# Chunk sums and outputs of an S5 scan: which operand is stationary

## The chip, the cores and the metric

The kernel runs on one core of a Trainium2 chip. The metric is device time in microseconds, from one launch to its end; a kernel's time is the median of several runs.

## The reference

A trunk of two layers works on 256 tokens of width 2048. Each layer normalises the stream, projects it, and feeds four branches: an S5 state-space layer (A), a gated DeltaNet (B), grid attention (C) and cross-attention into 256 memory tokens (M). Each branch is gated, projected back and merged; one output projection and a residual add end the layer.

The S5 branch has 48 groups of 16 channels, each with 64 complex states, and runs over the tokens forwards and backwards:

```
bu = einsum("blgp,gnp->blgn", u, bb)            # complex: bb_re, bb_im
s  = associative_scan(s_t = lam * s_(t-1) + bu_t, reverse=reverse)
y  = einsum("blgn,gpn->blgp", s_re, c_re) - einsum("blgn,gpn->blgp", s_im, c_im)
...
y = y_forward + y_backward + d * u
y = gelu(y);  y = y * sigmoid(y @ w_glu + b_glu)
```

## The kernel before

**The stream of large matmuls.** Most of the time goes to weight matrices that come from memory in chunks of 128 x 1024 (512 KB). Each chunk is split into a high and a low part, the high part by ScalarE (`hiN`, `hiT`) and the low part by VectorE (`loN`, `loT`), and TensorE multiplies three combinations of high and low parts into an accumulator (`acc`). Units of kind N have 512 moving columns and units of kind T have 256. The splits are issued two chunks ahead (`AHEAD = 2`), and a list (`ORDER`) fixes the sequence of the units in each layer.

**The order around it.** All engines get their instructions in an order worked out when the program is built. Small pieces of work are generators ("fibers"). After every few large matmuls, `tick` (line 530) lets those fibers go on whose data are ready by a model clock; `_time` (line 393) is the price list of that clock. On the chip each engine then works its own list in order and waits on semaphores.

**S5 in chunks.** The 256 tokens are cut into 32 chunks of 8. A group's 16 channels and 8 tokens make 128 rows, so that `ut` holds for each of 48 groups a 128 x 32 tile (rows by chunks). Twelve blocks have four groups each. The fiber `s5_fiber` (line 1458) goes through these steps in each layer:

1. `chunk_sums` (line 1473): for each block, the contribution of every chunk to the states: 128 rows of `ut` against a 128 x 256 matrix `W` for each group (64 states, two directions, real and imaginary parts), loaded from `Bd`. The result is copied into `Sx`, the states.
2. A recurrence over the 32 chunks on VectorE.
3. `outputs` (line 1524): for each block and group, three 128 x 128 matrices: `ct[0]` and `ct[1]` (loaded from `Cd`) meet the states `sy`, and `w0` (loaded from `Wd`) meets `ut`; the sum is copied to `yo`.
4. `yo` goes through memory into another layout, then GELU, and the units of the GLU, whose operand is called `sy` too.

Before the change the chunks are the stationary operand, 32 columns wide, and four groups share the array in four column tiles (`tile_position=(0, 32 * g)`), each writing 32 partitions of a PSUM bank; the matrices stream as the moving operand, 256 columns in the chunk sums and 128 in the outputs. So chunks come out on partitions. ScalarE copies the bank to a scratch tile, TensorE transposes it (`T`, line 662; two transposes for a block of chunk sums, one for a block of outputs), and ScalarE copies the transposed bank to `Sx` or `yo`.

In the profile all instructions bear line 379, where a helper records them, so they are told apart by their tiles. Both matmuls with `ut` appear as `bank<-scr,s5u`, those of the outputs with the states as `bank<-scr,scr`, transposes as `bank<-consts,...`. The DeltaNet's and S5's preparation use `bank<-scr,scr` and `bank<-scr,UA` too.

Of the kernel before, what the change touches and what calls it, by code (L numbers as in the profile page):

```python
# [11 lines left out]
AF = mybir.ActivationFunctionType  # L12
# [404 lines left out]
class Builder:  # L417
# [1040 lines left out]
    def s5_fiber(self, l):  # L1458
        nc = self.nc
        V, S, PE = self.V, self.S, self.PE  # L1460
        aux = 1 - l % 2
        yield from self.wait(("u", l))
        yield from self.wait(("pM", l))
        yield from self.wait(("C", l))
        yield from self.wait(("prep", l))
        Sx = self.slot(f"act{aux}0", "s5s", [128, 2, G_SSM, 33])
        ut = self.slot(f"act{aux}2", "s5u", [128, G_SSM, 32])
        for j in range(8):
            nc.sync.dma_start(out=ut[16 * j:16 * j + 16], in_=self.Ud[:, j, :].rearrange("(g i) c -> i g c", i=16))
        V.memset(Sx[:, :, :, 0:1], 0.0)  # L1470
        yield 7

        def chunk_sums(blocks):

            for b in blocks:
                gs = slice(4 * b, 4 * b + 4)
                W = yield from self.take(self.scr, 2)
                for hf in range(2):
                    nc.sync.dma_start(out=W[hf], in_=self.Bd[b][:, hf])
                yield 4  # L1480
                bank = yield from self.get(self.banks)
                for g in range(4):
                    PE.matmul(bank[32 * g:32 * g + 32, 0:256], ut[:, 4 * b + g, :], W[g // 2][:, (g % 2) * 256:(g % 2 + 1) * 256],
                              start=True, stop=True, tile_position=(0, 32 * g))
                self.scr.put(W[1])
                e = W[0]
                yield 1
                S.activation(out=e[:, 0:256], in_=bank[:, 0:256], func=AF.Copy)
                self.banks.put(bank)
                yield max(0, self.LAG + 1)  # L1490
                bank = yield from self.get(self.banks)
                for i in range(2):
                    self.T(bank[:, 128 * i:128 * i + 128], e[:, 128 * i:128 * i + 128])
                self.scr.put(e)
                yield 1
                src = bank[:, 0:256].rearrange("p (r g c) -> p r g c", r=2, c=32)
                S.activation(out=Sx[0:64, :, gs, 1:33], in_=src[0:64], func=AF.Copy)
                S.activation(out=Sx[64:128, :, gs, 32:0:-1], in_=src[64:128], func=AF.Copy)
                self.banks.put(bank)
                self.done(("sums", l))  # L1500

        self.expect(("sums", l), 12)
        for i in range(3):
            self.spawn(chunk_sums(range(i, 12, 3)))
        yield from self.wait(("sums", l))

        t = yield from self.get(self.scr)
        v = [t[:, 96 * i:96 * i + 96].rearrange("p (r g) -> p r g", r=2) for i in range(2)]
        tt = lambda o, a, b, op: V.tensor_tensor(out=o, in0=a, in1=b, op=op)
        lre, lim = self.lam8[:, 0:1, :].to_broadcast([128, 2, G_SSM]), self.lam8[:, 1:3, :]  # L1510
        for c in range(31):
            s0, s1 = Sx[:, :, :, c], Sx[:, :, :, c + 1]
            tt(v[0], s0, lre, ALU.mult)
            tt(v[1], s0[:, ::-1], lim, ALU.mult)
            tt(s1, s1, v[0], ALU.add)
            tt(s1, s1, v[1], ALU.add)
            yield 0
        self.scr.put(t)
        self.mark(("states", l))

        yo = self.slot(f"act{aux}3", "s5o", [128, G_SSM, 32])
        self.expect(("yo", l), 12)

        def outputs(blocks):
            for b in blocks:
                gs = slice(4 * b, 4 * b + 4)
                *ct, w0, w1 = yield from self.take(self.scr, 4)
                nc.sync.dma_start(out=w0, in_=self.Wd[:, 0, gs, :].rearrange("p g c -> p (g c)"))
                nc.sync.dma_start(out=w1, in_=self.Wd[:, 1, gs, :].rearrange("p g c -> p (g c)"))
                for i in range(2):  # L1530
                    nc.sync.dma_start(out=ct[i], in_=self.Cd[b][:, i])
                yield 6
                V.tensor_tensor(out=w0, in0=w0, in1=w1, op=ALU.add)
                sy = w1[:, 0:256].rearrange("p (r g c) -> p r g c", r=2, g=4)
                S.activation(out=sy[0:64], in_=Sx[0:64, :, gs, 0:32], func=AF.Copy)
                S.activation(out=sy[64:128], in_=Sx[64:128, :, gs, 31::-1], func=AF.Copy)
                yield self.LAG
                bank = yield from self.get(self.banks)
                for i in range(3):
                    for g in range(4):  # L1540
                        a = sy[:, i, g] if i < 2 else ut[:, 4 * b + g]
                        m = (ct[0], ct[1], w0)[i][:, g * 128:(g + 1) * 128]
                        PE.matmul(bank[32 * g:32 * g + 32, 0:128], a, m, start=i == 0, stop=i == 2, tile_position=(0, 32 * g))
                self.scr.put(*ct, w0)
                yield 0
                y1 = w1[:, 256:384]
                S.activation(out=y1, in_=bank[:, 0:128], func=AF.Copy)
                self.banks.put(bank)
                yield self.LAG
                bank = yield from self.get(self.banks)  # L1550
                self.T(bank[:, 0:128], y1)
                self.scr.put(w1)
                yield 1
                S.activation(out=yo[:, gs], in_=bank[:, 0:128].rearrange("p (g c) -> p g c", c=32), func=AF.Copy)
                self.banks.put(bank)
                self.done(("yo", l))

        self.spawn(outputs(range(0, 12, 2)))
        yield 6
        self.spawn(outputs(range(1, 12, 2)))  # L1560
        yield from self.wait(("yo", l))
        yield 1
        for j in range(8):
            nc.sync.dma_start(out=self.Yd[:, j, :].rearrange("(g o) c -> o g c", o=16), in_=yo[16 * j:16 * j + 16])
        yield 4

        Y = self.slot(f"act{aux}2", "s5y", [128, 6, 256])
        sy = self.slot(f"act{aux}0", "sy", [128, 6, 2, 256], F32R)
        nc.sync.dma_start(out=Y, in_=self.Yd.rearrange("(m p) j c -> p m (j c)", p=128))
        V.tensor_scalar(out=self.hbg, in0=self.sm(l, "b_glu"), scalar1=0.5, scalar2=None, op0=ALU.mult)  # L1570
        yield 8
        def gelu(m):
            s = yield from self.get(self.scr)
            y = Y[:, m:m + 2, :].rearrange("p m c -> p (m c)")
            S.activation(out=s, in_=y, func=AF.Square)
            yield 3
            V.tensor_scalar(out=s, in0=s, scalar1=0.044715, scalar2=1.0, op0=ALU.mult, op1=ALU.add)
            tt(s, s, y, ALU.mult)
            yield 3
            S.activation(out=s, in_=s, func=AF.Tanh, scale=math.sqrt(2.0 / math.pi))  # L1580
            yield 1
            V.scalar_tensor_tensor(out=y, in0=s, scalar=1.0, in1=y, op0=ALU.add, op1=ALU.mult)
            self.scr.put(s)
            yield 2
            S.activation(out=sy[:, m:m + 2, 0, :], in_=Y[:, m:m + 2, :], func=AF.Copy, scale=0.5)
            yield 5
            V.scalar_tensor_tensor(out=sy[:, m:m + 2, 1, :], in0=Y[:, m:m + 2, :], scalar=0.5,
                                   in1=sy[:, m:m + 2, 0, :].bitcast(F32), op0=ALU.mult, op1=ALU.subtract)
            self.done(("gelu", l))

        self.expect(("gelu", l), 3)
        for m in range(0, 6, 2):
            self.spawn(gelu(m))
        yield from self.wait(("gelu", l))
        self.sY = Y
        self.acts[("sy", l)] = [sy[:, 0:4], sy[:, 4:6]]
        self.expect(("A", l), 3)
        self.mark(("sy", l, 0))
        self.mark(("sy", l, 1))
        if l + 1 < DEPTH:  # L1600
            yield from self.wait(("B", l))
            self.spawn(self.s5_prep(l + 1), self.PREP_RANK[1])
# [276 lines left out]
```

## Time and profile before

| | us |
|---|---|
| median of 3 runs | 2280.83 (2280.21 to 2281.92) |
| the profiled run, its own time | 2280.38 |
| span of the profiled run, first to last instruction | 2278.6 |
| TensorE busy | 2228.1 |
| VectorE busy | 1700.7 |
| ScalarE busy | 1242.9 |
| mean granted clock of TensorE | 0.995 |

The busy time of an engine is the union of its instructions' times. Matmuls overlap their neighbours: the record of one begins before the one ahead of it has ended, so what a matmul costs is read from the distance between starts. PE is TensorE's matmul, PEld its weight load, DVE VectorE, ACT ScalarE.

### The profile page before, as it was taken

Reading aid. Unit: us, or ns where it says so; the run is one execution under the profiler, and the core shown is the slowest. Engines: PE = TensorE matmul, PEld = TensorE weight load, DVE = VectorE, ACT = ScalarE, POOL = GpSimd, SP = SyncE. Lnnn points to the kernel's source line nnn. Section 1 sums busy time; section 2 is a strip of 40 time slices with the busy share of each in tenths; the row PEclk is TensorE's granted clock in tenths of the full one; section 3 lists DMA queues with packets and bytes.
Section 4 is the critical chain, followed back from the end, with each engine's and each line's share of the span. In section 5 each row is a group of like instructions: output and inputs, shape, how many; then the busy total and the mean of one; then the engine's idle time right before and its main releaser. Section 6 shows DMA issues by size and latency. Waiting matters only on the chain.

```text
span 2278.6 us, 39516 instructions
## 1 busy us (share of the span) xinstructions
PE 2228.1 (98%) x14684; PEld 1930.3 (85%) x14684; DVE 1700.7 (75%) x2824; ACT 1242.9 (55%) x2176; POOL 89.8 (4%) x153
## 2 busy tenths in 40 slices
PE   6999999999999999999999999999999999999997
PEld 6988988988988888798789988898888887989886
DVE  6898887867859955889788858788646995566664
ACT  7645566465464454655665555666446445455443
POOL 0000000001000000000000000100000000000000
PEclk9999999999999999999999999999999999999999
DMA  6776678655775597778776786545478557877774
GB/s 247 250 246 214 229 247 280 203 189 190 183 264 197 185 322 259 252 230 293 266 228 206 244 288 210 191 169 205 166 196 279 199 197 277 263 253 258 231 245 139
DMA packets 245135, 523.42 MB, mean 230 GB/s; under 512 B 59320, under 2 KB 111032, under 8 KB 244304
## 3 DMA queue, kind: packets, MB, share of 16 engines
q1 hardware_dynamic: 218400, 471.41, 62.6%
q10 hardware_dynamic: 21952, 36.80, 4.5%
q0 software_dynamic: 4592, 12.69, 1.7%
q8 instruction: 117, 1.92, 0.3%
q14 instruction: 74, 0.61, 0.1%
HBM read 468.21 MB, written 65.18 MB: 234 GB/s over the span
## 4 chain that ended last, share of the span: by engine, by line
PE 89%; DVE 4%; DMA 2%; ACT 2%; issue 1%; SPq 0%; POOL 0%; ACTq 0%; POOLq 0%; DVEq 0%
PE acc L379 80%; PE bank L379 10%; DVE loT L379 2%; DVE hT L379 1%; DVE scr L379 1%; DMA Cd<-scr 1%; SPq L379 0%; DMA s5y<-Yd 0%; DVE dnx L379 0%; DMA xm<-x 0%; ACT hiT L379 0%; ACT scr L379 0%; DMA scr<-oTC 0%; DMA rawT<-wpack 0%; DMA Bd<-scr 0%
## 5 line engine op out<-in xcount | busy, mean ns | idle before, releaser
L379 ACT ACTIVATE hiN<-rawN 128x1024 fp32r<-128x1024 f32 x480 | 508.3, 1060 | 508.8 <-PE acc L379 431.5
L379 DVE TENSOR_TENSOR loN<-rawN,hiN 128x1024 fp32r<-128x1024 f32 x480 | 584.0, 1220 | 267.5 <-ACT hiN L379 266.1
L379 PE MATMUL acc<-hiN,xT 128*128 128x512 f32 x2432 | 619.3, 394 | 1.7 <-DVE hT L379 1.7
L379 PEld LDWEIGHTS acc<-hiN,xT 128*128 128x128 f32 x2432 | 449.6, 188 | 96.8 <-issue 5.9
L379 PE MATMUL acc<-xT,hiT 128*128 128x256 f32 x3392 | 444.8, 281 | 9.7 <-ACT gt L379 3.8
L379 PEld LDWEIGHTS acc<-xT,hiT 128*128 128x128 f32 x3392 | 413.3, 189 | 21.3 <-issue 11.3
L379 DVE TENSOR_TENSOR loT<-rawT,hiT 128x1024 fp32r<-128x1024 f32 x240 | 288.5, 1207 | 156.0 <-ACT hiT L379 151.4
L379 ACT ACTIVATE hiT<-rawT 128x1024 fp32r<-128x1024 f32 x240 | 250.3, 1048 | 182.6 <-PE acc L379 131.1
L379 PE MATMUL acc<-loN,xT 128*128 128x512 f32 x1216 | 337.1, 393 | 0.0
L379 PEld LDWEIGHTS acc<-loN,xT 128*128 128x128 f32 x1216 | 225.0, 188 | 46.3 <-issue 1.2
L379 PE MATMUL acc<-xT,loT 128*128 128x256 f32 x1696 | 239.6, 281 | 0.0
L379 PEld LDWEIGHTS acc<-xT,loT 128*128 128x128 f32 x1696 | 215.1, 190 | 2.6 <-issue 2.5
L379 ACT ACTIVATE scr<-bank 128x128 f32<-128x128 f32 (+6 forms) x324 | 105.7, 333 | 146.1 <-PE bank L379 122.6
L379 PE MATMUL acc<-hiN,y 128*128 128x512 f32 x640 | 161.5, 393 | 0.8 <-DVE scr L379 0.8
L379 PEld LDWEIGHTS acc<-hiN,y 128*128 128x128 f32 x640 | 118.5, 188 | 27.0 <-ACT hiN L379 1.8
L379 PE MATMUL acc<-hiN,mT 128*128 128x512 f32 x512 | 129.7, 393 | 1.3 <-ACT hiN L379 1.3
L379 DVE TENSOR_TENSOR dnx<-dnx 32x30 f32<-32x30 f32 (+9 forms) x360 | 114.6, 318 | 10.0
L379 PEld LDWEIGHTS acc<-hiN,mT 128*128 128x128 f32 x512 | 94.9, 188 | 21.5 <-ACT hiN L379 1.8
L379 PE MATMUL acc<-loN,y 128*128 128x512 f32 x320 | 88.7, 393 | 0.0
L379 DVE TENSOR_TENSOR scr<-scr,scr 128x512 f32<-128x512 f32 (+4 forms) x132 | 77.4, 590 | 2.4
L379 DVE SCALAR_TENSOR_TENSOR hT<-acc,small,hT 128x254 f32<-128x254 f32 (+1 forms) x144 | 69.1, 480 | 3.8
L379 PE MATMUL acc<-loN,mT 128*128 128x512 f32 x256 | 70.5, 393 | 1.3 <-DVE loN L379 1.3
(187 smaller groups left out, 2155.3 us busy)
## 6 DMA issues: line engine op xcount, KB each, us to landing
rawN<-wpack SPq DMA_DIRECT2D x480, 512.0 KB, 3.9
rawT<-wpack SPq DMA_DIRECT2D x234, 512.0 KB, 4.2
Bd<-scr ACTq DMA_DIRECT2D x48, 256.0 KB, 4.4
Cd<-scr SPq DMA_DIRECT2D x48, 256.0 KB, 4.7
Wd<-Kd SPq DMA_DIRECT2D x32, 384.0 KB, 6.1
scr<-Bd SPq DMA_DIRECT2D x48, 256.0 KB, 5.7
scr<-Wd SPq DMA_DIRECT2D x48, 256.0 KB, 5.1
scr<-Cd SPq DMA_DIRECT2D x48, 256.0 KB, 5.6
```

The costliest lines, as they stand in the source:

```text
L379: o = f(*args, **kw)
```

## The change

In both steps the operands change places. The matrices become the stationary operand, 128 columns wide on the full array, and the 32 chunks of a group the moving operand. The chunk sums take eight matmuls for a block instead of four, the outputs twelve as before; each writes 32 columns of a bank over all 128 partitions. The result then has the layout of `Sx` and `yo`: the copy to scratch, the transposes and the second bank go, and scratch tiles are given back right after the matmuls. The copies into `Sx` and `yo`, the loads and everything else stay.

```diff
                 bank = yield from self.get(self.banks)
                 for g in range(4):
-                    PE.matmul(bank[32 * g:32 * g + 32, 0:256], ut[:, 4 * b + g, :], W[g // 2][:, (g % 2) * 256:(g % 2 + 1) * 256],
-                              start=True, stop=True, tile_position=(0, 32 * g))
-                self.scr.put(W[1])
-                e = W[0]
-                yield 1
-                S.activation(out=e[:, 0:256], in_=bank[:, 0:256], func=AF.Copy)
-                self.banks.put(bank)
-                yield max(0, self.LAG + 1)
-                bank = yield from self.get(self.banks)
-                for i in range(2):
-                    self.T(bank[:, 128 * i:128 * i + 128], e[:, 128 * i:128 * i + 128])
-                self.scr.put(e)
+                    for i in range(2):
+                        PE.matmul(bank[:, (4 * i + g) * 32:(4 * i + g + 1) * 32],
+                                  W[g // 2][:, (g % 2) * 256 + 128 * i:(g % 2) * 256 + 128 * i + 128], ut[:, 4 * b + g, :],
+                                  start=True, stop=True)
+                self.scr.put(*W)
                 yield 1
...
                 bank = yield from self.get(self.banks)
-                for i in range(3):
-                    for g in range(4):
+                for g in range(4):
+                    for i in range(3):
                         a = sy[:, i, g] if i < 2 else ut[:, 4 * b + g]
                         m = (ct[0], ct[1], w0)[i][:, g * 128:(g + 1) * 128]
-                        PE.matmul(bank[32 * g:32 * g + 32, 0:128], a, m, start=i == 0, stop=i == 2, tile_position=(0, 32 * g))
-                self.scr.put(*ct, w0)
-                yield 0
-                y1 = w1[:, 256:384]
-                S.activation(out=y1, in_=bank[:, 0:128], func=AF.Copy)
-                self.banks.put(bank)
-                yield self.LAG
-                bank = yield from self.get(self.banks)
-                self.T(bank[:, 0:128], y1)
-                self.scr.put(w1)
+                        PE.matmul(bank[:, 32 * g:32 * g + 32], m, a, start=i == 0, stop=i == 2)
+                self.scr.put(*ct, w0, w1)
                 yield 1
```

## Rows read from the trace of the kernel before

**Rows 1.** The page's busy table: busy us, share of the span, instructions.

```profile
PE 2228.1 (98%) x14684; PEld 1930.3 (85%) x14684; DVE 1700.7 (75%) x2824; ACT 1242.9 (55%) x2176; POOL 89.8 (4%) x153
```

**Rows 2.** The chain that ended last, shares of the span by engine.

```profile
PE 89%; DVE 4%; DMA 2%; ACT 2%; issue 1%; SPq 0%; POOL 0%; ACTq 0%; POOLq 0%; DVEq 0%
```

**Rows 3.** Busy by stretch, clock, DMA: chunk sums, four S5 stretches' sum, 622 us.

```profile
632.00:676.00 44.00, 44.00 (x418) 37.13 (x417) 19.93 (x37) 31.66 (x82) 3.02 (x3) 1.00 0.80 272
...
sum 255.00, PE 252.26 PEld 215.13 DVE 136.88 ACT 153.94 POOL 6.43; mean PE 63.06 PEld 53.78 DVE 34.22 ACT 38.49 POOL 1.61
...
622.00:632.00 10.00, 7.43 (x124) 6.83 (x125) 7.84 (x14) 6.64 (x17) 0.00 (x0) 0.66 0.88 315
```

**Rows 4.** Waits of TensorE: us in total, times, longest us.

```profile
PE bank L379 <- ACT scr L379: 3.3, 3, 2.4
```

**Rows 5.** Timeline of TensorE at a block of chunk sums: start us, us.

```profile
1736.94 1.07 PE L379 MATMUL acc<-xT,loT 128*128 128x256 f32 x8
1737.85 0.38 PE L379 MATMUL bank<-consts,scr 128*128 128x128 f32 x2
...
1739.95 0.40 PE L379 MATMUL acc<-xT,loT 128*128 128x256 f32 x2
1740.28 0.64 PE L379 MATMUL bank<-scr,s5u 128*32 128x256 f32 x8
1740.85 0.96 PE L379 MATMUL acc<-xT,loT 128*128 128x256 f32 x6
1741.64 0.38 PE L379 MATMUL bank<-consts,scr 128*128 128x128 f32 x2
```

**Rows 6.** Timeline of TensorE at a block of outputs.

```profile
825.78 1.30 PE L379 MATMUL acc<-hiN,y 128*128 128x512 f32 x5
826.91 0.39 PE L379 MATMUL acc<-loN,y 128*128 128x512 f32 x1
827.23 0.64 PE L379 MATMUL bank<-scr,scr 128*32 128x128 f32 x16
827.69 0.40 PE L379 MATMUL bank<-scr,s5u 128*32 128x128 f32 x8
828.02 0.96 PE L379 MATMUL acc<-loN,y 128*128 128x512 f32 x3
828.82 0.27 PE L379 MATMUL bank<-consts,scr 128*128 128x128 f32 x1
```

**Rows 7.** Timeline of TensorE where only large matmuls run.

```profile
700.24 1.98 PE L379 MATMUL acc<-hiN,xT 128*128 128x512 f32 x8
702.05 1.07 PE L379 MATMUL acc<-loN,xT 128*128 128x512 f32 x4
```

**Rows 8.** Groups by form, matmuls: busy us, mean ns of one, idle before.

```profile
L379 PE MATMUL bank<-scr,UA 128*128 128x128 f32 x192 | 24.5, 276 | 0.0
L379 PE MATMUL bank<-hT 128*128 128x512 f32 x48 | 22.6, 592 | 0.0
...
L379 PE MATMUL bank<-scr,s5u 128*32 128x256 f32 x192 | 15.7, 390 | 1.9 <-DMA scr<-Bd 1.9
```

**Rows 9.** Groups by form, weight loads.

```profile
L379 PEld LDWEIGHTS bank<-consts,scr 128*128 128x128 f32 x388 | 46.8, 140 | 13.5 <-issue 2.8 <-ACT scr L379 2.3 <-DVE scr L379 1.0
...
L379 PEld LDWEIGHTS bank<-scr,UA 128*128 128x128 f32 x192 | 23.7, 191 | 1.4 <-ACT scr L379 0.2 <-issue 0.2
...
L379 PEld LDWEIGHTS bank<-scr,s5u 128*32 128x32 f32 x384 | 9.8, 109 | 5.7 <-DMA scr<-Bd 2.5 <-issue 1.2
```

**Rows 10.** Timeline of TensorE, sixteen float32 passes on the full array.

```profile
641.98 1.95 PE L379 MATMUL bank<-scr,UA 128*128 128x128 f32 x16
```

**Rows 11.** Timeline of TensorE, the first large matmuls after a wait (in brackets).

```profile
919.40 2.09 PE L379 MATMUL acc<-hiN,y 128*128 128x512 f32 x8 [0.82 <-DVE scr L379]
```

**Rows 12.** The GLU's operand, layer 0: ns min/median/max, first and last start.

```profile
L379 PE MATMUL acc<-sy,hiT x72: 276/276/386, 949.5 to 962.5; 128*128 128x256 f32 x72
...
L379 DVE SCALAR_TENSOR_TENSOR sy<-s5y,sy x3: 683/684/686, 928.8 to 940.2; 128x512 fp32r<-128x512 f32 x3
```

## The prediction

> **What bounds the kernel now.** I read the page's busy table first. TensorE is the engine to look at: busy 2228 of 2278.6 us [rows 1]. A busy share can hide a waiting engine, so the next view is the chain that ended last: 89% of it is TensorE [rows 2]. Then the four stretches in which the change lives (chunk sums and outputs, each in two layers). Over their 255.0 us TensorE is busy 252.3 us, ScalarE, which loses work in this change, 153.9 us [rows 3]: there are 2.7 us, no more, in which added TensorE work could disappear. The list of waits agrees: of TensorE's waits the one that the removed steps could have caused, on a scratch tile that ScalarE writes, is 3.3 us in the whole run, 2.4 us of it in one piece [rows 4]. So the question is only how much TensorE time a block of four groups takes before and after. Time that TensorE gains or loses here goes to the end of the kernel nearly one for one.
>
> **What a block costs now.** The reader should not add up durations, because these overlap; the cost of a small group is what it adds to the stream of large matmuls around it. In the chunk sums [rows 5]: from 1739.95 to 1741.64 are 1.69 us, which hold 2 + 6 large matmuls and one group of chunk sums (eight records). The eight large matmuls from 1736.94 to 1737.85 without a group take 0.91 us. The group costs 1.69 - 0.91 = 0.78 us. The eight records last 0.64 us together and one lasts 0.39 us [rows 5, 8], so they start within 0.25 us, and more than half of the price is getting into and out of the four column tiles. The two transposes last 0.38 us together and one lasts 0.27 us [rows 5, 6], so one comes 0.11 us behind the other; two cost 0.22 us. In the outputs [rows 6]: from 825.78 to 828.82 are 3.04 us with 5 + 1 + 3 large matmuls and one group (16 + 8 records). Large matmuls with 512 columns step at (702.05 - 700.24) / 8 = 0.226 us [rows 7], nine of them 2.04 us; the group costs 1.00 us, its one transpose 0.11 us. Together a block costs 0.78 + 0.22 + 1.00 + 0.11 = 2.11 us, and the 24 blocks (12 in each layer) 50.6 us. All of that goes.
>
> **What a block costs after.** Chunk sums: 4 groups x 2 halves = 8 matmuls with a 128-column stationary operand and 32 moving columns. Outputs: 4 x 3 = 12 of them. One float32 matmul is two records of weight load and stream: 2 layers x 12 blocks x 4 = 96 matmuls of the chunk sums stand as 192 records [rows 8]. So there are 16 + 24 = 40 passes a block, 960 in all. No row shows a pass with 128 stationary and 32 moving columns, and its price decides everything.
> From below, its stream: a float32 record of 512 columns takes 592 ns, one of 128 columns 276 ns [rows 8], which is 0.82 ns a column and 26 ns for 32 columns. Before it stands its weight load. Loads of 128 columns take 191 ns and loads of 32 columns 109 ns [rows 9]: 0.85 ns a column, so 128 columns occupy the load path for some 109 ns, the rest being latency. That a load really costs this when no stream covers it is seen after a wait: eight large matmuls last 2.09 us there and 1.98 us elsewhere [rows 11, 7], 0.11 us more. From above: the nearest row has the same stationary operand and four times the moving columns, 16 passes in 1.95 us, so one every (1.95 - 0.276) / 15 = 0.112 us [rows 10]; a pass with fewer columns can't be slower, unless load and stream stop overlapping. I take 0.112 us: at 128 columns load (0.109) and stream (0.105) are equally long, and shortening the stream leaves the load. 40 x 0.112 = 4.48 us a block, 107 us for all.
> The Trainium skill, "TensorEngine Tiling (Array Packing)", section Instruction Overhead, speaks the other way: a matmul has about 60 cycles of overhead, so that one with few columns costs what 60 columns cost. At 2.4 GHz that is an estimate of 25 ns a pass, by which the time would come out near 2253 us; it does not count the weight load, and no row here shows a pass so short with 128 stationary columns. The same page, section Performance Considerations, advises for at most 32 columns to make the narrow side stationary and to tile the columns, which is what the change undoes; the two prices here, 2.11 and 4.48 us a block, are on its side.
>
> **The rest of the change.** ScalarE loses two copies a block (a 128x256 and a 128x128 one); it has room in all four stretches, so this is worth nothing but the wait above, at most 3.3 - 2.4 = 0.9 us [rows 3, 4]; I take 0.5 us. The loads of the next block are issued when scratch tiles come back, and these come back earlier, since no copy and transpose hold one; nothing is added to SP's queue. A copy out of PSUM now waits for the longer group, and behind it on ScalarE stand the splits of the weights, on which TensorE waits in turn; they are issued two chunks ahead, and one chunk lasts 12 x 0.226 = 2.7 us of TensorE, so a delay of some 1 us a group is covered. Without that cover it would be up to 1 us for each of 48 groups. The next thing that could be late is the GLU, which waits for the outputs: its operand is ready at 940.2 + 0.7 us and its first matmul starts at 949.5 us [rows 12], and the work between is TensorE's own, so a longer TensorE stage moves both. The plan by which the program orders its instructions prices a new matmul at 0.08 us (line 393), so a block at 0.64 + 0.96 us instead of 0.67 + 0.83 us; the order should change little, and I allow 10 us to either side for it.
>
> **Sum.** The profiled run took 2280.38 us, 1.8 us more than its span, and the median is 0.45 us above it. 2280.4 - 50.6 + 107.1 - 0.5 = 2336.4 us, so 2336 us, slower by 2.4%. With passes at 0.109 us it is 2334 us.
>
> **Rivals.**
> Short streams win, faster than before: if a load were taken ahead while earlier passes run, so that loads no longer follow each other one at a time, a pass would cost its stream, 26 ns. Then 960 x 0.026 = 25 us replace 50.6 us: 2254 us. It decides below 2.11 / 40 = 53 ns a pass. For it: a load is seen to run beside a stream, since both fill the 0.112 us of a pass [rows 10]. Against it: the 0.11 us after a wait [rows 11], and that a load grows with its columns [rows 9]. Chance 0.03. The skill's rule on overhead, above, ends in the same place.
> Loads as short as those of the transposes: these take 140 ns, not 191 [rows 9], so 51 ns less, 58 ns a pass. 960 x 0.058 = 55.7 us: 2285 us, about the bound of what can be told. Against it: the transposes are another kind of matmul, the plain ones all show about 190 ns. Chance 0.05.
> Load and stream one after the other, 109 + 26 = 135 ns: 129.6 us, 2359 us. Against it: at 128 columns they overlap, or the 16 passes would take twice as long [rows 10]. Chance 0.05.
> The clock falls: TensorE's granted clock was at 0.66 in the ten microseconds from 622 us [rows 3], after waits, that is 6.8 us at 1.2 instead of 2.4 GHz and 3.4 us lost. Passes that stream for 26 of 112 ns leave the array idle for most of some 2 us at a time. One such spell for every two blocks of outputs would cost 12 x 3.4 = 41 us: 2377 us. Against it: between the groups stand full matmuls, and the clock read 1.00 all through the chunk sums of layer 0 [rows 3]. Chance 0.03.
> That it does nothing would need idle TensorE time to take it in, and there are 2.7 us [rows 3].
>
> **How the numbers follow.** The forecast has a chance of 0.84, with a range of its own from 2324 to 2350 us (0.109 to 0.115 us a pass and 10 us for the order). The faster rival is 0.03, and a shift of the order on top of the cheap loads adds 0.01 to faster and 0.02 to same; a difference under 0.2%, 4.6 us, cannot be told. Slower holds the rest, 0.94. The range goes from 2322 us to 2359 us, up to the serial case, and leaves out the two short-pass cases, the clock and a tail of the forecast, together some 0.17.
>
> **What the profile after would show.** Rows of TensorE with 128 stationary and 32 moving columns, 384 with the chunk operand and 384 with the states, stepping at 0.11 us; 16 of them 1.8 us, 24 of them 2.7 us. The rows with 32 stationary columns and 256 moving ones gone, transposes of scratch tiles down from 388 to 316. The stretches of chunk sums longer by about 0.8 us a block and those of outputs by 1.6 us, TensorE's waits no longer than now, the granted clock at 1.00 in them. A step of 0.03 or 0.06 us between these passes, a low clock in the stretches, or new waits for the weight splits would make the prediction wrong.

## The result and the profile after

The changed kernel takes 2332.66 us, the median of 4 runs (2331.24 to 2335.05), beside 2280.52 us for the kernel before (4 runs): a ratio of 1.0234, interval 1.0222 to 1.0247, so 52.1 us or 2.3% slower. The run that was profiled took 2331.24 us, its span is 2329.5 us and the mean granted clock 0.995.

The page of the changed kernel, first the busy table (busy us, share of the span, instructions), then the shares of the chain that ended last, answers to [rows 1, 2]:

```profile
PE 2283.4 (98%) x14804; PEld 2010.9 (86%) x14804; DVE 1699.9 (73%) x2824; ACT 1232.6 (53%) x2128; POOL 88.3 (4%) x153
...
PE 91%; DVE 4%; DMA 2%; ACT 2%; issue 1%; SPq 0%; ACTq 0%; POOL 0%; POOLq 0%; DVEq 0%
```

TensorE is busy 55.3 us longer than before and the span is 50.9 us longer. ScalarE lost 10.3 us of work, and the end moved the other way. The groups by form (busy us, mean ns of one, idle before) show the passes that have come in [rows 8, 9]:

```profile
L379 PE MATMUL bank<-s5u,scr 128*128 128x32 f32 x576 | 82.2, 273 | 0.6 <-DMA scr<-Bd 0.6
L379 PE MATMUL bank<-scr,scr 128*128 128x32 f32 x384 | 56.8, 271 | 0.0
L379 PE MATMUL bank<-consts,scr 128*128 128x128 f32 x316 | 49.2, 274 | 0.9 <-DVE scr L379 0.7 <-DVE memT L379 0.2
L379 PEld LDWEIGHTS bank<-s5u,scr 128*128 128x128 f32 x576 | 73.9, 192 | 0.9 <-DMA scr<-Bd 0.7
```

576 + 384 = 960 passes, and 72 transposes fewer (388 to 316). The mean of one, 273 ns, is no price: 960 of them would be 261 us. The price is in the starts. The timeline of TensorE at one block of chunk sums, and at one of outputs (start us, us, instruction, count), answers to [rows 5, 6]:

```profile
662.41 0.39 PE L379 MATMUL acc<-xT,loT 128*128 128x256 f32 x2
662.64 1.87 PE L379 MATMUL bank<-s5u,scr 128*128 128x32 f32 x16
664.34 0.95 PE L379 MATMUL acc<-xT,loT 128*128 128x256 f32 x6
665.13 0.38 PE L379 MATMUL bank<-consts,scr 128*128 128x128 f32 x2
...
842.41 0.87 PE L379 MATMUL acc<-xT,hiT 128*128 128x256 f32 x6
843.11 0.53 PE L379 MATMUL bank<-scr,scr 128*128 128x32 f32 x4
843.48 0.39 PE L379 MATMUL bank<-s5u,scr 128*128 128x32 f32 x2
843.70 0.61 PE L379 MATMUL bank<-scr,scr 128*128 128x32 f32 x4
844.15 0.39 PE L379 MATMUL bank<-s5u,scr 128*128 128x32 f32 x2
844.37 0.61 PE L379 MATMUL bank<-scr,scr 128*128 128x32 f32 x4
...
845.71 1.40 PE L379 MATMUL acc<-xT,hiT 128*128 128x256 f32 x10
846.94 1.07 PE L379 MATMUL acc<-xT,loT 128*128 128x256 f32 x8
```

The chunk sums: 665.13 - 662.41 = 2.72 us hold eight large matmuls, 0.91 us by [rows 5], and one group: 1.81 us. The outputs: 846.94 - 842.41 = 4.53 us hold sixteen large matmuls, 1.82 us, and one group: 2.71 us. Inside, six passes take 844.37 - 843.70 = 0.67 us, 0.112 us each. The medians over the groups of the trace, worked out the same way, are 1.794 and 2.688 us, together 4.48 us a block, which is 40 x 0.112 us; before they were 0.773 + 0.228 + 0.995 + 0.119 = 2.115 us. Each median is good to 0.02 us, which is the doubt in the step of the large matmuls around it. 24 x (4.48 - 2.115) = 56.8 us. That is the whole loss of span, and 6 us more than it.

The waits of TensorE (us in total, times, longest us) come to 31.8 us over the whole list, beside 36.0 us before. Its four largest lines, none of them new:

```profile
PE bank L379 <- ACT xm L379: 13.4, 1, 13.4
PE acc L379 <- DVE xT L379: 3.8, 3, 2.3
PE bank L379 <- ACT scr L379: 3.3, 2, 2.4
PE acc L379 <- DVE hT L379: 3.1, 2, 1.6
```

The third answers to [rows 4]: it is as long as it was.

### The profile page after: what moved, and what is told of

Its sections match the earlier page's. It is cut to its first block, busy times and chain, and to the rows that moved or that the text cites. A ratio compares the mean times of both kernels' runs of the same rounds, so it can differ in the third digit from the quotient of the medians.

```text
span 2329.5 us, 39721 instructions
## 1 busy us (share of the span) xinstructions
PE 2283.4 (98%) x14804; PEld 2010.9 (86%) x14804; DVE 1699.9 (73%) x2824; ACT 1232.6 (53%) x2128; POOL 88.3 (4%) x153
## 3 DMA queue, kind: packets, MB, share of 16 engines
q8 instruction: 118, 1.93, 0.3%
## 4 chain that ended last, share of the span: by engine, by line
PE 91%; DVE 4%; DMA 2%; ACT 2%; issue 1%; SPq 0%; ACTq 0%; POOL 0%; POOLq 0%; DVEq 0%
PE acc L379 79%; PE bank L379 12%; DVE loT L379 1%; DVE scr L379 1%; DVE hT L379 1%; DMA Kd<-scr 0%; SPq L379 0%; DVE loN L379 0%; DMA xm<-x 0%; ACT hiT L379 0%; DMA rawN<-wpack 0%; ACT scr L379 0%; DMA rawT<-wpack 0%; DMA scr<-Bd 0%; DVE xm L379 0%
## 5 line engine op out<-in xcount | busy, mean ns | idle before, releaser
L379 ACT ACTIVATE hiN<-rawN 128x1024 fp32r<-128x1024 f32 x480 | 508.6, 1060 | 523.4 <-PE acc L379 439.7
L379 DVE TENSOR_TENSOR loN<-rawN,hiN 128x1024 fp32r<-128x1024 f32 x480 | 583.7, 1219 | 274.9 <-ACT hiN L379 268.6
L379 PE MATMUL acc<-hiN,xT 128*128 128x512 f32 x2432 | 617.5, 393 | 1.6 <-DVE hT L379 1.6
L379 PEld LDWEIGHTS acc<-hiN,xT 128*128 128x128 f32 x2432 | 450.3, 188 | 95.0 <-issue 3.9
L379 PE MATMUL acc<-xT,hiT 128*128 128x256 f32 x3392 | 442.2, 281 | 7.9 <-DVE xT L379 3.8
L379 PEld LDWEIGHTS acc<-xT,hiT 128*128 128x128 f32 x3392 | 412.7, 189 | 11.7 <-DVE xT L379 4.7
L379 DVE TENSOR_TENSOR loT<-rawT,hiT 128x1024 fp32r<-128x1024 f32 x240 | 288.3, 1206 | 180.9 <-ACT hiT L379 175.6
L379 ACT ACTIVATE hiT<-rawT 128x1024 fp32r<-128x1024 f32 x240 | 249.8, 1048 | 182.9 <-PE acc L379 143.8
L379 PE MATMUL acc<-loN,xT 128*128 128x512 f32 x1216 | 337.4, 393 | 0.0
L379 PEld LDWEIGHTS acc<-loN,xT 128*128 128x128 f32 x1216 | 225.0, 188 | 46.1 <-issue 1.1
L379 PE MATMUL acc<-xT,loT 128*128 128x256 f32 x1696 | 238.9, 281 | 0.0
L379 PEld LDWEIGHTS acc<-xT,loT 128*128 128x128 f32 x1696 | 214.8, 190 | 0.8 <-issue 0.7
L379 PE MATMUL acc<-hiN,y 128*128 128x512 f32 x640 | 162.2, 393 | 0.4 <-ACT hiN L379 0.4
L379 ACT ACTIVATE scr<-bank 128x128 f32<-128x128 f32 (+6 forms) x276 | 90.1, 333 | 125.9 <-PE bank L379 106.3
L379 PEld LDWEIGHTS acc<-hiN,y 128*128 128x128 f32 x640 | 118.7, 188 | 25.4 <-ACT hiN L379 1.1
L379 PE MATMUL acc<-hiN,mT 128*128 128x512 f32 x512 | 128.9, 392 | 0.7 <-ACT hiN L379 0.7
L379 DVE TENSOR_TENSOR dnx<-dnx 32x30 f32<-32x30 f32 (+9 forms) x360 | 114.6, 318 | 10.6 <-DMA dnx<-Sd 0.5
L379 PEld LDWEIGHTS acc<-hiN,mT 128*128 128x128 f32 x512 | 95.1, 188 | 20.5 <-ACT hiN L379 1.1
L379 PE MATMUL acc<-loN,y 128*128 128x512 f32 x320 | 88.8, 393 | 0.0
L379 PE MATMUL bank<-scr,scr 128*32 128x128 f32 (+4 forms) x1272 | 87.0, 249 | 0.9 <-ACT scr L379 0.9
L379 PEld LDWEIGHTS bank<-scr,scr 128*32 128x32 f32 (+3 forms) x1272 | 71.8, 137 | 14.5 <-issue 8.6
L379 PE MATMUL bank<-s5u,scr 128*128 128x32 f32 x576 | 82.2, 273 | 0.6 <-DMA scr<-Bd 0.6
```

What stands on the lines that cost most here:

```text
L379: o = f(*args, **kw)
```

## Experiments

The theory: a pass costs what loading 128 stationary columns takes, 0.112 us, and the time follows from the number of passes. The rivals: the stream or the number of instructions counts as well; the granted clock; the order that the program's plan makes of the instructions. "Before" and "changed" say which kernel an edit starts from. Where an edit alters what the plan pays for a matmul, the order of the instructions changes with it; the text says where that is so.

### The load cut into four column tiles (from changed)

```diff
-                        PE.matmul(bank[:, 32 * g:32 * g + 32], m, a, start=i == 0, stop=i == 2)
+                        for q in range(0, 128, 32):
+                            PE.matmul(bank[q:q + 32, 32 * g:32 * g + 32], m[:, q:q + 32], a, start=i == 0, stop=i == 2,
+                                      tile_position=(0, q))
```

The chunk sums are cut in the same way. Same products, same layout; four loads of 32 columns stand side by side in place of one of 128.

> Each new matmul is cut into four of 32 stationary columns, one in each column tile, with the same streams of 32 columns. If the weight load sets the price (theory), the four loads run side by side and a round of four records costs about 0.03 us: 16 rounds in the chunk sums and 24 in the outputs, each with some 0.35 us for getting in and out of the tiles, 0.8 + 1.0 us a block against 2.11 us before, so about 2274 us. If instead every record has a price of its own, whatever its load (rival), four times as many records cost at least as much as now: 2330 us or more.

Measured: 2295.29 us (6 runs), ratio to before 1.0082 (1.0066 to 1.0098). The groups fell to 0.899 us (chunk sums) and 1.165 us (outputs), 2.06 us a block instead of 4.48, with four times as many records. So neither the products nor the number of instructions made the change dear, but passes that load 128 columns on the full array. No run loads fewer columns on the undivided array, so another cost of a full-array pass is not split from its load. By the groups the kernel should have come to 2332.66 - 24 x 2.42 = 2275 us; it is 21 us above that. The plan prices the four pieces at 0.12 us together instead of 0.08, so the order differs too. TensorE's waits are 50.6 us in all, 18.8 us more than in the changed kernel. The list of waits and the timeline (idle before an instruction and what ended it in brackets) show most of them:

```profile
PE bank L379 <- issue: 18.3, 10, 3.3
```

```profile
652.28 1.50 PE L379 MATMUL bank<-scr,UA 128*128 128x128 f32 x12
653.71 1.00 PE L379 MATMUL bank<-s5u,scr 128*32 128x32 f32 x92
657.53 0.51 PE L379 MATMUL bank<-s5u,scr 128*32 128x32 f32 x36 [2.83 <-issue]
```

In the middle of a run of small records TensorE stops for 2.83 us with nothing that the profile names to wait for. Ten such stops make 18.3 us, a line that the changed kernel's list does not have. The DMA packets in the trace point to the supply of instructions. Packets of 16 KB of the kind "instruction" come over queue q8, 118 of them in the changed kernel and more here (packets, MB, share):

```profile
q8 instruction: 140, 2.29, 0.4%
```

For each of the ten stops, and for an eleventh of 1.2 us before a large matmul, one such packet begins 2.2 to 2.6 us before TensorE goes on and lands 1.1 to 1.5 us before it; in the changed kernel no packet of q8 is followed by such a stop. That fits all eleven, but no run takes the cause away.

The clock has a part as well. Over two stretches with many of these groups it read 0.90 and 0.94 (the third number from the end of each line); in the changed kernel it read 1.00 and 0.98 over the same stretches. That is at most 50 x 0.10 + 90 x 0.04 = 8.6 us, part of it inside the stops. Waits and clock together cover the 21 us.

```profile
630.00:680.00 50.00, 40.13 (x997) 36.49 (x997) 18.41 (x48) 25.82 (x72) 3.02 (x3) 0.90 0.64 215
825.00:915.00 90.00, 82.44 (x1303) 73.12 (x1303) 47.66 (x55) 43.45 (x67) 0.00 (x0) 0.94 0.82 270
```

### 64 columns streamed instead of 32 (from changed)

```diff
-                        PE.matmul(bank[:, 32 * g:32 * g + 32], m, a, start=i == 0, stop=i == 2)
+                        PE.matmul(bank[:, 64 * g:64 * g + 64], m, a, start=i == 0, stop=i == 2)
...
-                S.activation(out=yo[:, gs], in_=bank[:, 0:128].rearrange("p (g c) -> p g c", c=32), func=AF.Copy)
+                S.activation(out=yo[:, gs], in_=bank[:, 0:256].rearrange("p (g c) -> p g c", c=64)[:, :, 0:32], func=AF.Copy)
```

The moving operand takes the 32 columns that follow as well, in the chunk sums too; their products are never read.

> As the changed kernel, but every new matmul streams 64 columns; the second 32 go to parts of the bank that nobody reads. If the load of 128 columns sets the pass (theory), the step stays 0.112 us and the time 2333 us. If load and stream add up (rival), 960 passes get 0.026 us each: 2358 us.

Measured: 2322.01 us (4 runs), ratio 1.0190 (1.0177 to 1.0203). One block of chunk sums in its timeline:

```profile
661.92 0.95 PE L379 MATMUL acc<-xT,hiT 128*128 128x256 f32 x6
662.71 1.89 PE L379 MATMUL bank<-s5u,scr 128*128 128x64 f32 x16
664.41 0.95 PE L379 MATMUL acc<-xT,hiT 128*128 128x256 f32 x6
```

From the first of the 16 passes to the next large matmul are 1.70 us with 64 columns and 664.34 - 662.64 = 1.70 us with 32. Over all groups the medians are 1.794 and 2.691 us, beside 1.794 and 2.688. Twice the stream costs nothing. That the kernel is even 10.7 us faster than the changed one was expected by neither side. Its order is not that of the changed kernel: the plan prices a matmul by its moving columns, 4 x 64 / 2400 + 0.027 = 0.134 us instead of 0.080, and TensorE's instructions follow each other otherwise from the first chunk sums on. Its waits add up to 26.5 us, 5.3 less than the changed kernel's, and the clock's fall of 3.4 us at 892.9 us (below) is missing, at most 1.7 us; the other 3.7 us are not placed. The step of a pass is read inside the groups and does not depend on the order.

### One part alone

The chunk sums of the changed kernel with the outputs of the kernel before, and the other way round. The core of the two edits, from changed, the first for the chunk sums alone, the second for the outputs alone:

```diff
+                        PE.matmul(bank[32 * g:32 * g + 32, 0:128], a, m, start=i == 0, stop=i == 2, tile_position=(0, 32 * g))
...
+                self.T(bank[:, 0:128], y1)
```

```diff
+                    PE.matmul(bank[32 * g:32 * g + 32, 0:256], ut[:, 4 * b + g, :], W[g // 2][:, (g % 2) * 256:(g % 2 + 1) * 256],
+                              start=True, stop=True, tile_position=(0, 32 * g))
...
+                    self.T(bank[:, 128 * i:128 * i + 128], e[:, 128 * i:128 * i + 128])
```

For the chunk sums alone:

> Only the chunk sums are turned round. Theory: 16 passes of 0.112 us replace 0.78 + 0.22 us, 24 x 0.79 = 19 us, so 2299 us. Rival, that the missing 5 us of the whole change were saved in this stage (a shorter way through the chunk sums): 2294 us.

For the outputs alone:

> Only the outputs are turned round. Theory: 24 passes of 0.112 us replace 1.00 + 0.11 us, 24 x 1.58 = 38 us, so 2318 us. Rival, that the missing 5 us of the whole change were saved in this stage: 2313 us.

Measured, beside 2278.54 us before on that chip: the sums alone 2300.34 us, +21.8 (ratio 1.0096, 1.0083 to 1.0109); the outputs alone 2309.63 us, +31.1 (1.0134, 1.0121 to 1.0147). The groups price them at 24 x (1.794 - 1.001) = 19.0 us and 24 x (2.688 - 1.114) = 37.8 us. The two parts together make 52.9 us, as the whole does (52.1), so each acts by itself, as far as the spread of the runs lets one say (the sums alone took 2296.85 to 2304.82 us). The microseconds that the whole falls short of its groups appear with the outputs, which fall short by 6.7 us; the list of waits gives 4.0 us of it (32.0 beside 36.0), the rest is not placed.

### The output matmuls done twice (from changed)

```diff
+                for g in range(4):
+                    for i in range(3):
+                        a = sy[:, i, g] if i < 2 else ut[:, 4 * b + g]
+                        m = (ct[0], ct[1], w0)[i][:, g * 128:(g + 1) * 128]
+                        PE._e.matmul(bank[:, 32 * g:32 * g + 32], m, a, start=i == 0, stop=i == 2)
```

The plan does not see the second set, which writes the same values again.

> The changed kernel with the twelve output matmuls of every block done twice, the second time over the first. The order of all other instructions stays as it is, since the plan is not told of the repeats. If a pass costs 0.112 us of TensorE's time and nothing hides it (theory), 24 x 24 passes add 64 us: 2397 us. If part of such work goes into time that TensorE would have waited (rival for the missing 5 us), it adds less, 55 us or under.

Measured: 2458.85 us (4 runs), ratio 1.0782 (1.0763 to 1.0801). 24 x 24 x 0.112 = 64.5 us were added by the theory, and 126 us came. The timeline shows the step from one pass to the next change (L379 is the first set, L1541 the second):

```profile
818.51 0.61 PE L379 MATMUL bank<-scr,scr 128*128 128x32 f32 x4
818.96 0.39 PE L379 MATMUL bank<-s5u,scr 128*128 128x32 f32 x2
...
821.61 1.04 PE L1541 MATMUL bank<-scr,scr 128*128 128x32 f32 x4
822.46 0.61 PE L1541 MATMUL bank<-s5u,scr 128*128 128x32 f32 x2
```

Four passes take 0.45 us in the first set and 0.85 us in the second: 0.112 us a pass, then 0.213. The windows over the two stretches of outputs (span; us and count on PE, PEld, DVE, ACT and POOL; granted clock; DMA share; GB/s) name the reason, a clock of 0.80 and 0.82 in the mean:

```profile
800.00:1000.00 200.00, 200.00 (x1284) 186.01 (x1283) 59.83 (x83) 57.72 (x107) 1.83 (x2) 0.80 0.46 152
2000.00:2160.00 160.00, 160.00 (x1019) 150.61 (x1019) 45.98 (x48) 41.84 (x68) 1.08 (x1) 0.82 0.48 154
```

So the clock rival, which the changed kernel shows in one spell of 3.4 us only, is real when more of these passes follow each other. The next experiment takes it away.

### The same passes twice, each streaming 128 columns (from the last)

```diff
-                        PE._e.matmul(bank[:, 32 * g:32 * g + 32], m, a, start=i == 0, stop=i == 2)
+                        PE._e.matmul(bank[:, 128 * g:128 * g + 128], m, a, start=i == 0, stop=i == 2)
```

This is the core of the edit. Both sets of outputs stream 128 columns, of which 32 are read; the plan is given the price of the narrow ones, so that the order stays. In the two traces TensorE's 15380 matmul records follow each other in the same order.

> As the run with doubled outputs, instruction for instruction in the same order, but every output matmul, the first set and the repeat, streams 128 columns instead of 32; the other 96 go to parts of the bank that nobody reads. If the low clock of that run came from the short streams (theory), the granted clock stays near 0.995 and the repeat costs its passes alone, 576 x 0.112 = 64 us: 2397 us, in spite of four times the streamed columns. If the clock falls whatever the streams are, or the repeat is dear for another reason (rival): 2450 us or more.

Measured: 2401.76 us (4 runs), ratio 1.0540 (1.0524 to 1.0555): 57 us less than with 32 columns. Timeline and windows of the same places:

```profile
822.43 0.61 PE L1548 MATMUL bank<-scr,scr 128*128 128x128 f32 x4
822.88 0.39 PE L1548 MATMUL bank<-s5u,scr 128*128 128x128 f32 x2
823.10 0.61 PE L1548 MATMUL bank<-scr,scr 128*128 128x128 f32 x4
```

```profile
800.00:1000.00 200.00, 198.70 (x1443) 179.32 (x1442) 94.30 (x128) 77.75 (x131) 2.15 (x3) 1.00 0.62 209
2000.00:2160.00 160.00, 160.00 (x1043) 145.50 (x1042) 73.58 (x79) 64.51 (x85) 0.00 (x0) 1.00 0.61 203
```

Four times the stream, the same 0.112 us a pass, the clock at 1.00, and the total where the theory put it (2397). This pair shows both halves: the stream does not set the pass, and the 57 us were the clock.

### The plan's price alone

The plan orders the instructions by estimated durations. From before, the column-tiled matmuls are priced half as much again; from changed, the new matmuls at what they cost (0.224 us for two passes) instead of 0.08:

```diff
+            if cols == 32 and rows == 128:
+                share *= 1.5
```

```diff
+            if n == 32 and cols == 128:
+                return 0.224
```

For before, priced:

> The kernel before with nothing changed but the plan's price of a matmul in four column tiles, times 1.5; the engines do the same work in another order. If the missing 5 us come from another order (theory), this alone moves the time by some us, 2273 to 2288 us. If the order hardly matters (rival), it stays within 1 us of before.

For changed, priced:

> The changed kernel with the plan told the measured price of a new matmul, 0.224 instead of 0.08 us. TensorE's work is the same. Theory: within 8 us of 2333 us, by the order alone. Rival, that the change was slow because the plan was wrong about its price: it comes back by 20 us or more.

Measured, beside 2279.63 us: before, priced, 2270.91 us, ratio 0.9961 (0.9947 to 0.9975), 8.7 us gained with not one operation changed. TensorE's waits are 30.1 us instead of 36.0. The clock can give the rest: over 600 to 650 us and 950 to 1000 us it read 0.93 and 0.97 before and 1.00 in both here, worth up to 5.0 us, less up to 1.7 us for one new fall of 3.4 us at 426.4 us. Changed, priced, 2360.78 us, ratio 1.0353 (1.0339 to 1.0367), 28 us above the changed kernel. The true price makes it worse: the plan now puts up to 48 passes in a row. Its timeline and windows in the chunk sums of the second layer:

```profile
1740.73 7.80 PE L379 MATMUL bank<-s5u,scr 128*128 128x32 f32 x48 [1.24 <-DMA scr<-Bd]
1748.35 3.76 PE L379 MATMUL acc<-xT,hiT 128*128 128x256 f32 x16
1751.91 1.91 PE L379 MATMUL acc<-xT,loT 128*128 128x256 f32 x8
```

```profile
1740.00:1780.00 40.00, 39.27 (x235) 39.30 (x236) 13.91 (x26) 13.34 (x30) 0.00 (x0) 0.66 0.59 209
```

48 passes at 0.112 us are 5.4 us; they took 7.6 us, and the 16 large matmuls behind them 3.56 us instead of 1.82. The clock stands at 0.66 in these 40 us. TensorE had also waited 1.24 us for a load just before, so this place alone would not tell the wait from the passes; the doubled outputs, where the clock fell with no wait between the two sets, do.

To see whether the 28 us are the clock or the order, the same prices with 64 columns streamed in the chunk sums and 128 in the outputs, by the edits shown above. TensorE's records follow each other in the same order in both traces.

> As the changed kernel with the measured price in its plan, in the same order, but with 64 columns streamed in the chunk sums and 128 in the outputs. If its 28 us above the changed kernel come from the clock (theory), most of them come back: 2325 to 2340 us with a mean clock of 0.99 or more. If they come from the order itself (rival): 2355 us or more.

Measured: 2329.89 us (4 runs), ratio 1.0221 (1.0200 to 1.0243), 31 us below the narrow one. Its windows there; the narrow kernel's clock read 1.00 in the first of them and 0.66 in the second, as shown:

```profile
1720.00:1740.00 20.00, 18.14 (x118) 17.98 (x117) 8.41 (x14) 7.85 (x14) 0.00 (x0) 0.74 0.82 310
1740.00:1780.00 40.00, 40.00 (x356) 39.98 (x354) 25.05 (x58) 18.17 (x33) 0.00 (x0) 1.00 0.60 204
```

The clock is back at 1.00 in the 40 us; one fall of 10.2 us stays at 1727.3 us. So the 28 us were the clock. What the order does beyond that is small beside it: with the clock back, this kernel is 2.8 us below the changed one. The kernel with 64 columns (2322.01 us) has a third order and no such fall, so its 8 us are no measure of this order.

### The other direction: two blocks in one way through the column tiles (from before)

If the price of before lies mostly in getting into and out of the column tiles, two blocks in one go save one way in and out.

```diff
-                bank = yield from self.get(self.banks)
-                for g in range(4):
-                    PE.matmul(bank[32 * g:32 * g + 32, 0:256], ut[:, 4 * b + g, :], W[g // 2][:, (g % 2) * 256:(g % 2 + 1) * 256],
-                              start=True, stop=True, tile_position=(0, 32 * g))
+                two = yield from self.take(self.banks, 2)
+                for n in range(2):
+                    for g in range(4):
+                        PE.matmul(two[n][32 * g:32 * g + 32, 0:256], ut[:, 4 * (b + n) + g, :],
+                                  W[2 * n + g // 2][:, (g % 2) * 256:(g % 2 + 1) * 256],
+                                  start=True, stop=True, tile_position=(0, 32 * g))
```

This is the core of the edit. The outputs go two blocks at a time as well, in one bank.

> The kernel before, but chunk sums and outputs of two blocks follow each other without leaving the column tiles, and so share one way in and out. A group costs 0.78 and 1.00 us, of which 0.35 us are the way in and out: 24 times 0.35 us are saved, 8 us, so 2272 us. If the loads of twice as many scratch tiles at once come late (rival), waits eat it: 2280 us or more.

Measured: 2264.35 us (5 runs), ratio 0.9932 (0.9919 to 0.9946): 15.3 us faster than before. Its timeline at two blocks of chunk sums:

```profile
659.34 0.95 PE L379 MATMUL acc<-xT,hiT 128*128 128x256 f32 x6
660.23 1.07 PE L379 MATMUL bank<-scr,s5u 128*32 128x256 f32 x16
661.23 1.45 PE L379 MATMUL acc<-xT,hiT 128*128 128x256 f32 x10
```

661.23 - 659.34 = 1.89 us less 0.68 us for six large matmuls is 1.21 us for two blocks, which one at a time cost 2 x 0.773 = 1.55 us. Two blocks of outputs cost 1.65 us beside 2 x 0.995. Each pair saves 0.34 us: 24 pairs of both steps, 8.2 us. Of the other 7 us, 5.1 are in the waits (30.9 us instead of 36.0), and up to 2 us in the clock, which read 0.97 over 600 to 650 us where it read 0.93 before.

A further run was expected so:

> A second look at the kernel before with blocks in pairs: 2264 us again, its groups at 1.65 us for two blocks of outputs and 1.20 us for two of chunk sums.

What ran there was the kernel of the pairs itself, at the plan's own prices, so it is a second look at it and says nothing of a price: 2263.62 us in one run, beside 2278.46 before.

The two gains put together, pairs and the column-tiled matmuls priced half as much again:

> The kernel before with blocks in pairs and, in its plan, the price of a matmul in column tiles times 1.5. If the gain of the other order (9 us) and that of the pairs (15 us) were independent, 2255 us; if an order that suits one is lost with the other, 2264 us or more. The groups themselves cost what they cost in pairs.

Measured: 2262.59 us (4 runs), ratio 0.9931 (0.9915 to 0.9948), beside 2278.21 before; the interval is about that of the pairs alone. The gains of order and pairs do not add up. This is the fastest version of the study, 70 us below the changed kernel.

## Why the prediction was right, and where its size was off

The forecast was 2336 us, the median came out at 2332.66, inside both ranges and on the side that held 0.94.

- **TensorE's time goes to the end nearly one for one: right.** The groups cost 56.8 us more, the span is 50.9 us longer, and the copies that ScalarE lost brought nothing.
- **What a block costs now, 2.11 us: right.** Medians over all groups give 2.115. That more than half of a group of chunk sums is the way into and out of the column tiles is too much: the pairs, which share one way, save 0.34 of 0.773 us, and 0.34 of 0.995 us in the outputs. The sum does not use that share. The Trainium skill, "TensorEngine Tiling (Array Packing)", section Key Properties, says that a change of tiling mode drains TensorE; that agrees with a price of 0.34 us for one way in and out, and the page gives no price.
- **What a pass costs after, 0.112 us: right, and it decides.** 16 and 24 passes take 1.79 and 2.69 us as forecast (1.8 and 2.7). That it is the load was an inference from equal times of load and stream at 128 columns. The experiments bear it out: 64 and 128 columns of stream cost what 32 do, and a load cut into four side by side brings a block to 2.06 us. In the changed kernel's chunk sums of layer 0 the weight loads are busy for 47.39 of 48.00 us (windows below), beside 37.13 of 44.00 before [rows 3]. The Trainium skill, "TensorE: Matmul & The Clock Gate", section LDWEIGHTS (loading the stationary operand), puts a load, in ns, at its columns divided by 1.2, an estimate of 107 ns here, near the step of 112 ns measured. The Trainium skill's rule on overhead, which the prediction set against it (25 ns a pass), comes to less than a quarter of that step; it does not count the load.
- **The wait worth 0.5 us: the term that was mis-sized.** The one wait that the removed copies caused, 0.58 us before two transposes at 1715.0 us, did go. But one of 0.91 us on another scratch tile came at 1910.1 us, and the waits on scratch tiles that ScalarE writes stayed at 3.3 us. What fell is other waits of TensorE, 4.2 us over the whole list: the load of the chunk matrices from 1.9 to 0.6 us, the GLU's gate from 3.8 to 2.7, and others. 2280.4 + 56.8 - 4.2 = 2333.0 us, and the profiled run took 2331.2; the last 1.8 us are not placed.
- **10 us for the order: needed.** The plan's price alone moved the kernel before by 8.7 us.
- **Counts.** The rows with the chunk operand are 576, not the 384 foretold: the outputs have one such matmul in three, 192 records, that were left out there (not in the 960 passes of the sum). The 384 with the states and the 316 transposes are as foretold.
- **The rivals.** Short streams, loads like those of the transposes, and load and stream in series are out: at the full clock the step is 0.112 us. New waits for the weight splits did not come: on `hiN`, `hiT` and `loN` TensorE waited 2.8 us, beside 3.5 us before. The clock is the one rival that is only nearly out. In the four stretches it read 1.00 but for one fall, in the outputs of layer 0, here in the timeline and the windows of the changed kernel:

```profile
891.82 0.61 PE L379 MATMUL bank<-scr,scr 128*128 128x32 f32 x4
892.27 0.39 PE L379 MATMUL bank<-s5u,scr 128*128 128x32 f32 x2
892.49 2.13 PE L379 MATMUL acc<-xT,hiT 128*128 128x256 f32 x10
```

```profile
632.00:680.00 48.00, 48.00 (x440) 47.39 (x439) 14.94 (x26) 23.83 (x58) 1.41 (x2) 1.00 0.69 230
820.00:915.00 95.00, 95.00 (x699) 90.02 (x699) 42.02 (x47) 41.67 (x76) 1.83 (x2) 0.98 0.76 250
1720.00:1780.00 60.00, 59.42 (x524) 59.26 (x522) 30.29 (x46) 27.67 (x48) 0.00 (x0) 1.00 0.91 260
1930.00:2020.00 90.00, 90.00 (x647) 84.08 (x647) 40.21 (x42) 38.82 (x64) 0.00 (x0) 1.00 0.74 248
```

After the 24 passes of a block, ten large matmuls step through 894.42 - 892.49 = 1.93 us instead of 1.23 us (846.94 - 845.71 above). The spell lasted 3.4 us; the kernel before had one as long at 968.1 us that the changed one has not, so the totals do not show it. The rival had the right kind of passes: with 128 columns streamed the clock stayed up. What kept its price away is the order: with its price of 0.08 us the plan put large matmuls between most blocks, and with 0.224 us, where it put up to 48 passes in a row, the same passes cost 28 us more.

Left open: 3.7 of the 10.7 us that the kernel with 64 columns gains, 2.7 of the 6.7 us by which the outputs alone fall short of their groups, and a run that would take the stops out of the cut loads.

## What to carry to other kernels

Before the operands of a small matmul change places to save transposes, count the passes and what loading their stationary columns takes: here a float32 pass with 128 stationary columns cost 0.112 us, whether 32, 64 or 128 columns streamed past them, and 40 of them replaced steps of 2.11 us a block, transposes included. Where a narrow side sits in column tiles, it is cheaper to send two blocks through in one go than to leave the tiles. And after any such edit look at the order and the clock, not only at the groups: a price in the plan moved one kernel by -9 us and another by +28 us.

## What the runs showed of the hardware that was not expected

- A run of passes with 128 stationary and 32 moving columns can lower the granted clock, and the large matmuls behind it pay too: 48 in a row took 7.6 us instead of 5.4, the next 16 large matmuls 3.56 us instead of 1.82. The same passes with 128 moving columns take no longer and kept the clock at 1.00 over the outputs; this was worth 57 us in one kernel and, with 64 and 128 columns, 31 us in another. Streaming columns that nobody reads made these two kernels faster.
- In runs of many very small records TensorE stopped: with 128 stationary columns cut into four tiles of 32 there are ten stops of up to 3.3 us, 18.3 us in all, for which the wait list names nothing. Each ends 1.1 to 1.5 us after a 16 KB packet of the kind "instruction" has landed on queue q8.
- Sharing one way into and out of the column tiles saved 0.34 us, as much as three passes on the full array take.
